# Rotating a matrix by 90 degrees: a new order of the output buffers, and a wait moved from TensorE to ScalarE

## The chip, the cores and the metric

The kernel runs on one core of one Trainium2 chip. The metric is the time of one execution on the device in microseconds (us), as the median of several runs. The engines that matter are TensorE (PE in the profile, with its weight loads as PEld), VectorE (DVE), ScalarE (ACT), GpSimd (POOL) and SyncE (SP). Transfers between the chip's main memory and the on-chip memory run on 16 DMA engines, which two queues share here: q1 holds what SyncE issues, q10 what ScalarE issues.

## The reference

The input `x` is a matrix of 8192 x 8192 float32 values, 268 MB, and `k` is 1. The result is the matrix turned by 90 degrees against the clock:

```
def reference(x, k):
    return np.rot90(x, k)
```

Element (r, c) of the input becomes element (8191 - c, r) of the output. There is no arithmetic: every value is read once and written once, but rows become columns.

## The kernel before, in words

**Tiling.** The input is cut into 16 macro tiles of 1024 rows by 4096 columns (`R`, `W`), counted by `kk`. A macro tile is loaded by 8 transfers of 128 full rows, 2 MB each (`m` counts loads over the whole run, 128 in all). It is written by 8 outputs (`n`, 128 in all), each 512 output rows by 1024 output columns, 2 MB each. `n % 8` is called the position of an output in its macro tile below.

**Path of the data.** A load lands in one of the buffers; VectorE copies it, reversed, into the `ring`, which holds one macro tile (63 slots of 128 x 512; a 64th piece, the corner, stays in its landing buffer). The copy of load t of the next macro tile overwrites the slots that output t of the present one has left. So VectorE, before it copies load m, waits until output m - 8 has been read out of the ring: `s_half` counts finished transposes on TensorE, `s_pool` finished outputs on GpSimd.

Outputs come by two ways. At positions 0, 2, 4 and 6 (`BY_PE`) TensorE transposes the 32 blocks of 128 x 128 into its accumulation memory `ps`, which has two halves of 128 x 2048, and ScalarE evicts them in three copies to an output buffer. At positions 1, 3, 5 and 7 (`moved`) VectorE transposes 32 x 32 blocks while it fills the ring, and the quarters of the blocks are moved to the output buffer by 16 copies: 2 by VectorE, 12 by GpSimd, 2 by ScalarE. The last of GpSimd's 12 waits for the other two engines' shares (`s_act`, `s_dve`). In the first and the last macro tile all outputs go by TensorE, and in the last but one position 7 does too.

**Buffers.** There are five buffers of 128 x 4096. After the start, numbers 0 and 1 (`LAND`) take loads in turn, and numbers 2, 3 and 4 (`OUTS`) take outputs. Which output takes which is said by `TURN`, one list for even macro tiles and one for odd ones. Eight outputs don't divide by three buffers, and the loops of VectorE, TensorE and GpSimd repeat every two macro tiles, so the order must repeat with 16 outputs. Read through, the lists before give a reuse distance (how many outputs back the same buffer was used) of 2 at position 0, 4 at position 1 and 3 elsewhere.

**Order of the work.** All orders and waits are written out by hand. SyncE issues the loads, each when the load two before has been taken out of its landing buffer (`taken`; for the last load of a macro tile this includes the corner, which TensorE transposes in the output at position 0). ScalarE issues every store right after the output's last eviction or move, and each store counts up `s_store` of its buffer. `room_for(wait, n)` waits until the last store from output n's buffer has landed. It is called by GpSimd, VectorE and ScalarE for outputs that are moved. For outputs of TensorE it is called by TensorE, ahead of the last transpose of the output's first part (`by_tensor`); ScalarE, which writes the buffer, is ordered behind it by `s_half`. ScalarE calls it itself only at position 7 (the corner) and for one output of the last macro tile.

Of the kernel before, what the change touches and what calls it, by code (L numbers as in the profile page):

```python
# [13 lines left out]
J = W // (G * P)  # L14
# [17 lines left out]
LAND = 2  # L32
OUTS = 3

LINE = 1024

TURN = [[1, 2, 0, 1, 2, 0, 1, 2], [1, 0, 2, 1, 0, 2, 1, 0]]
HEAD = 224


# [131 lines left out]
def kernel(tc: tile.TileContext, x: bass.AP, k: bass.AP, out: bass.AP):  # L172
# [7 lines left out]
    KK = len(macros)  # L180
    n_out = KK * J
# [17 lines left out]
    def in_quadrants(kk, j):  # L199
        return j not in by_pe(kk)  # L200

    moved = [in_quadrants(kk, js[0]) for kk, _, js, _ in outs]


    FIRST = [n_out - J, n_out - J + 1]
    parts, evicted, seen = {}, {}, 0
    for n, (kk, ts, js, blocks) in enumerate(outs):
# [4 lines left out]
        ends = [F // H, F - CH, F] if kk < KK - 1 else [F // H, end]  # L212
        if kk < KK - 1 and js[0] == J - 1:
            ends = [F // H, F // H + rows, F]
# [51 lines left out]
    def load_buf(m):  # L266
        if m < T:
            return m % (LAND + OUTS)
        return LAND + 2 if m == T else (m - T - 1) % LAND

    def out_buf(n):
        e = n - (KK * J - J)
        if e < 0:
            return LAND + TURN[n // J % 2][n % J]
        ends = [load_buf(n_load - 2)]
        ends += [LAND + i for i in range(OUTS)]
        ends += [load_buf(n_load - 1)]
        return ends[e % len(ends)]

    def once(e):  # L280
        seen = {}

        def wait(sem, n):
            if seen.get(sem, 0) < n:
                seen[sem] = n
                e.wait_ge(sem, n)

        return wait

    def room_for(wait, n):  # L290
        b = out_buf(n)
        stores = [i for i in range(n) if out_buf(i) == b]
        loads = [i for i in range(n_load) if load_buf(i) == b]
        if stores:
            wait(s_store[b], 16 * len(stores))
        elif loads:
            taken(wait, loads[-1])

    def taken(wait, m):
        kk, t = divmod(m, T)  # L300
        wait(s_rev, max(rev[m, j] for j in range(J)))
        if t == T - 1 and kk < KK - 1:
            wait(s_corner, kk + 1)  # L303
# [18 lines left out]
    for m in range(n_load):  # L322
        kk, t = divmod(m, T)
# [24 lines left out]
    def chunk(kk, t, js):  # L348
        if (kk, t, js[0]) == (KK - 1, T - 1, J - 1):
            return at(ring[:], 0, [[CH, 1], [1, CH]])  # L350
        places = [slot(kk, t, j) for j in js]
        assert max(places) < SLOTS
        return at(ring[:], places[0] * CH, [*strides(places, CH), [1, CH]])

    def moves(n, share):
        kk, ts, (j,), _ = outs[n]
        rows = len(ts) * P
        places = [slot(kk, t, j) for t in ts if (t, j) != (T - 1, J - 1)]
        ((step, tiles),) = strides(places, CH)
        for a, q in share:  # L360
            yield (
                at(
                    bufs[out_buf(n)][q * Q : q * Q + Q, :],
                    a * Q,
                    [[rows, G], [P, tiles], [1, Q]],
                ),
                at(
                    ring[a * Q : a * Q + Q, :],
                    places[0] * CH + q * Q,
                    [[P, G], [step, tiles], [1, Q]],  # L370
                ),
            )
# [19 lines left out]
    def load_in_turn(e, m, queue):  # L392
        if queue not in queues(m):
            return
        last = [i for i in range(m) if load_buf(i) == load_buf(m)]
        taken(e.wait_ge, last[-1])
        load(e, m, queue)
# [76 lines left out]
    def in_turn():  # L474
        for n in parts:
            if n == FIRST[0]:
                early, late = parts[n], parts[FIRST[1]]
                yield n, early[:2]
                yield FIRST[1], late[:1]
                yield n, early[2:]  # L480
                yield FIRST[1], late[1:]
            elif n != FIRST[1]:
                yield n, parts[n]

    def by_tensor(e):
        e.part(-1)
        wait = once(e)
        e.wait_ge(s_id, 2)
        used = {}
        for n, some in in_turn():  # L490
            kk, ts, js, blocks = outs[n]
            e.part(kk)
            rows = len(ts) * P
            order = [(part, f) for part in some for f in part[2]]
            if js[0] == 0 and kk < KK - 1:
                late = parts[n][-1]
                order.sort(key=lambda o: (o[0] == late, o[1] % rows, o[1]))
            last = dict(order)
            for part, f in order:
                _, h, cols = part  # L500
                j, off = blocks[f // rows]
                t = ts[f % rows // P]
                if kk < KK - 1 and js[0] == 0 and f == parts[n][-1][2][0]:
                    m = kk * T + T - 1
                    wait(s_rev, rev[m, J - 1])
                    wait(s_freed, kk)
                    for g in range(G):
                        i = e.transpose(
                            corner[:, g * P : g * P + P],
                            bufs[load_buf(m)][:, g * P : g * P + P],  # L510
                            ident,
                        )
                    i.then_inc(s_corner, 1)
                if n == KK * J - J and h:
                    wait(s_freed, KK - 1)
                if used.get(h, part) != part:
                    wait(s_ev, evicted[used[h][0]] + 1)
                wait(s_rev, rev[kk * T + t, j])
                if part == parts[n][0] and f == last[part] and n != FIRST[1]:
                    room_for(wait, n)  # L520
                to = cols.index(f) * P
                i = e.transpose(
                    ps[h][:, to : to + P],
                    chunk(kk, t, [j])[:, 0, off : off + P],
                    ident,
                )
                if f == last[part]:
                    i.then_inc(s_half, 1)
                    used[h] = part

    def by_scalar(e):
        e.part(-1)
        wait = once(e)
        e.wait_ge(s_id, 2)
        e.copy(scratch, ident[:, :1])
        for m in EARLY[LAND + OUTS :]:
            load_in_turn(e, m, nc.scalar)
        for n, (kk, ts, js, blocks) in enumerate(outs):
            e.part(kk)
            r0, c0 = macros[kk]  # L540
            rows = len(ts) * P
            b = out_buf(n)
            if moved[n] or n == FIRST[1] or (kk < KK - 1 and js[0] == J - 1):
                room_for(wait, n)
            todo = list(moves(n, pairs[BY_DVE + BY_POOL :])) if moved[n] else []
            for to, of in todo[:1]:
                e.copy(to, of)
            if kk < KK - 1 and js[0] == J - 1:
                e.wait_ge(s_corner, kk + 1)
                e.copy(  # L550
                    at(bufs[b][:], rows - P, [[rows, G], [1, P]]),
                    at(corner, 0, [[P, G], [1, P]]),
                ).then_inc(s_freed, 1)
            if moved[n]:
                for to, of in todo[1:]:
                    i = e.copy(to, of)
                i.then_inc(s_act, 1)
                e.wait_ge(s_pool, moved_until(n))
            else:
                for k, h, cols in parts[n]:  # L560
                    e.wait_ge(s_half, k + 1)
                    run, deep = len(cols) * P, 1
                    if cols[-1] - cols[0] >= run:
                        run = P * sum(f // rows == cols[0] // rows for f in cols)
                        deep = len(cols) * P // run
                    e.copy(
                        at(bufs[b][:], cols[0], [[rows, deep], [1, run]]),
                        at(ps[h][:], 0, [[run, deep], [1, run]]),
                    ).then_inc(s_ev, 1)
                e.wait_ge(s_ev, turned_until(n))  # L570
            groups = len(blocks)
            top = M - c0 - js[0] * CH - groups * P
            left = r0 + ts[0] * P
            e.dma_start(
                out=Place(out, top, groups * P, left, rows),
                in_=bufs[b][:, : groups * rows].rearrange("m (g f) -> m g f", f=rows),
            ).then_inc(s_store[b], 16)
# [12 lines left out]
    last = {out_buf(n): n for n in range(n_out)}  # L590
# [37 lines left out]
```

## Time and profile before

| | |
|---|---|
| median of 3 runs | 1261.35 us (1260.8 to 1262.37) |
| profiled execution | 1263.2 us, of which the profile's span is 1261.9 us |
| moved | 537.09 MB, mean 426 GB/s |
| queue q10 (stores and the first loads), share of 16 engines | 52.0% |
| queue q1 (loads) | 48.1% |
| GpSimd busy | 754.2 us (60%) |
| VectorE busy | 596.8 us (47%) |
| TensorE busy | 520.6 us (41%) |
| ScalarE busy | 391.0 us (31%) |
| TensorE waiting for a store | 297.8 us in 57 waits |
| GpSimd waiting for a store | 228.3 us in 41 waits |
| ScalarE waiting for a store | 52.5 us in 41 waits |
| a store of 2 MB, issue to landing (median) | 15.7 us |
| a load of 2 MB, issue to landing (median) | 15.8 us |

The profile shows one execution. Its slices cut the span in 40 equal parts; a window gives busy times of each engine in a stretch, with the number of instructions in brackets, then the clock granted to TensorE, the busy share of the 16 DMA engines and what they moved. A wait in brackets in the timeline is the idle time of an engine before an instruction, and behind the arrow stands what ended it. An instruction of the loops is put down to line 102 of the kernel, where a helper records all of them, so the groups are told apart by engine and tile name. The shares of the two queues add up to the whole span: an engine that is idle costs nothing unless it makes a queue run dry.

### The profile page before, as it was taken

What the parts mean: (1) busy time and instruction counts of PE and PEld (TensorE: products, weight loads), DVE (VectorE), ACT (ScalarE), POOL (GpSimd) and SP (SyncE); (2) the same over time, 40 slices, a digit from 0 to 9 for tenths busy, and PEclk for the clock granted to TensorE, in tenths of its full rate; (3) what the DMA queues carried; (4) which work ended last, traced back from release to release, by engine and by line L of the source; (5) the groups of instructions that cost most, each with busy time, mean ns of one, the idle gap of its engine ahead of it and who ended that gap; (6) DMA issues with size and microseconds to landing.
All of it is one profiled execution on the core that took longest, in us unless ns stands there. A gap on an engine that the chain in (4) does not pass through costs nothing.

```text
span 1261.9 us, 7238 instructions
## 1 busy us (share of the span) xinstructions
PE 520.6 (41%) x2388; PEld 436.2 (35%) x2388; DVE 596.8 (47%) x389; ACT 391.0 (31%) x339; POOL 754.2 (60%) x666
## 2 busy tenths in 40 slices
PE   1555444234433344433344344343443434434374
PEld 0444333233333233323233233332332333323364
DVE  2533555545455454554544555545555455454410
ACT  0333233222332333313323233232332322313254
POOL 0003566776668667686676766767767677677700
PEclk9975555656655556565666655555555555555577
DMA  9999999999999999999999999999999999999999
GB/s 398 420 428 423 410 430 412 430 429 413 431 427 428 431 430 428 431 431 428 430 431 430 428 430 431 430 428 431 430 428 430 431 430 428 431 430 428 429 421 385
DMA packets 36945, 537.09 MB, mean 426 GB/s; under 512 B 4160, under 2 KB 4160, under 8 KB 4160
## 3 DMA queue, kind: packets, MB, share of 16 engines
q10 hardware_dynamic: 19184, 278.93, 52.0%
q1 hardware_dynamic: 17744, 257.96, 48.1%
q8 instruction: 8, 0.13, 0.0%
q14 instruction: 9, 0.07, 0.0%
HBM read 268.44 MB, written 268.44 MB: 425 GB/s over the span
## 4 chain that ended last, share of the span: by engine, by line
DMA 75%; DVE 10%; issue 6%; ACT 4%; POOL 2%; PE 1%; ACTq 0%; DVEq 0%; SPq 0%; POOLq 0%
DMA buf<-in_x_dram 63%; DMA out_dram<-buf 12%; DVE ring L102 10%; ACT buf L102 4%; POOL buf L102 2%; PE ps L102 1%; DVE buf L102 1%; ACTq L102 0%; DVEq L99 0%; SPq L383 0%; SPq L411 0%; POOLq L149 0%; SPq L303 0%; POOLq L99 0%; SPq L406 0%
## 5 line engine op out<-in xcount | busy, mean ns | idle before, releaser
L102 POOL COPY buf<-ring 32x1024 f32<-32x1024 f32 (+1 forms) x660 | 753.5, 1142 | 437.6 <-DMA out_dram<-buf 228.3
L102 PE MATMUL ps<-head,ring 128*128 128x128 f32 x2328 | 507.8, 397 | 725.7 <-DMA out_dram<-buf 297.8
L102 PEld LDWEIGHTS ps<-head,ring 128*128 128x128 f32 x2328 | 423.4, 208 | 809.9 <-DMA out_dram<-buf 319.0
L102 ACT COPY buf<-ps 128x512 f32<-128x512 f32 (+3 forms) x227 | 277.8, 1288 | 796.3 <-POOL buf L102 459.9
L102 DVE COPY ring<-buf 128x2048 f32<-128x2048 f32 (+4 forms) x152 | 212.7, 1406 | 620.0 <-DMA buf<-in_x_dram 565.5
L102 DVE STREAM_TRANSPOSE ring<-buf 128x2048 f32<-128x2048 f32 (+1 forms) x112 | 246.3, 2199 | 0.0
L102 DVE COPY buf<-ring 32x1024 f32<-32x1024 f32 (+1 forms) x110 | 147.2, 1338 | 0.7
L102 ACT COPY buf<-ring 32x1024 f32<-32x1024 f32 (+1 forms) x110 | 111.7, 1016 | 57.8 <-DMA out_dram<-buf 47.7
L102 PE MATMUL ps<-head,buf 128*128 128x128 f32 x60 | 15.9, 420 | 0.0
L102 PEld LDWEIGHTS ps<-head,buf 128*128 128x128 f32 x60 | 13.0, 229 | 0.0
L102 DVE COPY buf<-buf 128x512 f32<-128x512 f32 x15 | 5.8, 386 | 0.0
L102 ACT ACT_TABLE_LOAD x1 | 1.3, 1283 | 3.4 <-PEq L411 3.4
L102 POOL MEMSET head<- 128x128 f32 x1 | 0.2, 204 | 2.9 <-POOLq L411 2.9
L102 POOL TENSOR_SCALAR_AFFINE_SELECT head<-head 128x128 f32<-128x128 f32 x1 | 0.3, 292 | 0.2 <-POOL head L102 0.2
L609 POOL MEMSET const-float32-0.0<- 128x1 f32 x1 | 0.1, 98 | 0.2 <-issue 0.2
L102 ACT COPY head<-head 128x1 f32<-128x1 f32 x1 | 0.2, 191 | 0.0
L609 POOL MEMSET const-bfloat16-1.0<- 128x1 bf16 x1 | 0.1, 101 | 0.0
L609 POOL MEMSET const-uint8-127<- 128x1 uint8 x1 | 0.1, 101 | 0.0
L609 POOL MEMSET const-float32-1.0<- 128x1 f32 x1 | 0.1, 98 | 0.0
## 6 DMA issues: line engine op xcount, KB each, us to landing
out_dram<-buf ACTq DMA_DIRECT2D x128, 2048.0 KB, 15.7
buf<-in_x_dram SPq DMA_DIRECT2D x121, 2048.0 KB, 15.8
buf<-in_x_dram ACTq DMA_DIRECT2D x3, 2048.0 KB, 16.9
buf<-in_x_dram SPq DMA_DIRECT2D x4, 1024.0 KB, 16.0
buf<-in_x_dram ACTq DMA_DIRECT2D x4, 1024.0 KB, 16.3
```

The lines of the kernel that those rows point to most:

```text
L102: i = getattr(e, self.name)(*self.args, **kwargs)
L609: nc = _bacc.Bacc("TRN2", target_bir_lowering=False, num_devices=1)
```

## The change

The lists in `TURN` are replaced. Read through, the new ones give distance 3 at positions 0 and 1, distance 2 at position 4, distance 4 at position 5 and 3 elsewhere. For outputs at position 4, in all macro tiles but the last (`tight`), `room_for` is no longer called by TensorE but by ScalarE, ahead of its first eviction of that output. In the last macro tile the three output buffers are taken in reverse order.

```
-TURN = [[1, 2, 0, 1, 2, 0, 1, 2], [1, 0, 2, 1, 0, 2, 1, 0]]
+TURN = [[1, 2, 0, 1, 0, 2, 1, 0], [2, 1, 0, 2, 0, 1, 2, 0]]
+TIGHT = 4
...
-        ends += [LAND + i for i in range(OUTS)]
+        ends += [LAND + i for i in reversed(range(OUTS))]
...
+    def tight(n):
+        return n < n_out - J and n % J == TIGHT
...
-                if part == parts[n][0] and f == last[part] and n != FIRST[1]:
+                if part == parts[n][0] and f == last[part] and n != FIRST[1] and not tight(n):
                     room_for(wait, n)
...
-            if moved[n] or n == FIRST[1] or (kk < KK - 1 and js[0] == J - 1):
+            if moved[n] or tight(n) or n == FIRST[1] or (kk < KK - 1 and js[0] == J - 1):
                 room_for(wait, n)
```

## The prediction

> **What bounds the kernel now.** I read the page's slices first, then busy time by windows, then the DMA queues in two short windows, then the timeline around them.
>
> Page, part 2 (40 slices of 31.5 us; DMA busy share, GB/s moved):
>
> ```profile
> DMA  9999999999999999999999999999999999999999
> GB/s 398 420 428 423 410 430 412 430 429 413 431 427 428 431 430 428 431 431 428 430 431 430 428 430 431 430 428 431 430 428 430 431 430 428 431 430 428 429 421 385
> ```
>
> DMA is busy throughout and moves about 430 GB/s wherever nothing disturbs it; 537.09 MB at 430 GB/s is 1249.0 us of the 1261.9 us span. So only the dips can be won: 12.9 us in all, start and end included. The windows place them (start:end, length, busy of PE, PEld, DVE, ACT, POOL, clock, DMA share, GB/s):
>
> ```profile
> 120.00:140.00 20.00, 12.35 (x55) 10.93 (x56) 8.87 (x6) 9.47 (x8) 7.84 (x8) 0.59 0.99 386
> 200.00:220.00 20.00, 12.07 (x54) 10.63 (x55) 9.49 (x7) 9.48 (x8) 12.05 (x11) 0.59 0.99 398
> 220.00:280.00 60.00, 18.48 (x80) 15.49 (x78) 30.90 (x21) 14.01 (x13) 43.35 (x39) 0.59 1.01 430
> 280.00:300.00 20.00, 12.39 (x57) 10.84 (x57) 9.90 (x6) 9.48 (x8) 11.42 (x10) 0.59 1.00 405
> 360.00:380.00 20.00, 12.47 (x57) 10.24 (x55) 9.76 (x6) 11.04 (x10) 11.99 (x12) 0.59 1.01 427
> 380.00:660.00 280.00, 108.10 (x470) 90.08 (x470) 143.65 (x92) 82.90 (x75) 198.36 (x176) 0.59 1.01 430
> ```
>
> Four dips, 78 to 80 us apart: the first outputs of macro tiles 1 to 4. Lost against 430 GB/s: 20 x (1 - 386/430) = 2.05 us, then 1.49, 1.16 and 0.14: 4.84 us. After 380 us there is none. The DMA share stands at 0.99 to 1.01 in a dip as outside it, so the share hides the loss and the GB/s shows it. Who stopped, by the queues (q10 carries the stores, q1 the loads), at 121.9 to 125.1 us and then at 127 to 131.4 us:
>
> ```profile
> q10 hardware_dynamic: 82, 1.33, 97.5%
> q1 hardware_dynamic: 1, 0.00, 0.0%
> ```
>
> ```profile
> q1 hardware_dynamic: 87, 1.43, 100.2%
> ```
>
> First the loads are dry and the stores alone run at 415 GB/s: almost nothing lost. Then the stores are dry, one load alone is in flight, and 324 GB/s flow: here the loss is made. The timeline names the cause (start, length, engine, operation, and in brackets the wait before):
>
> ```profile
> 122.60 0.69 PE L102 MATMUL ps<-head,ring 128*128 128x128 f32 x2 [9.17 <-DMA out_dram<-buf]
> 126.19 1.96 DVE L102 COPY ring<-buf 128x2048 f32<-128x2048 f32 x1 [9.16 <-PE ps L102]
> 126.84 0.55 ACTq L102 DMA_DIRECT2D out_dram<-buf  x1
> ```
>
> TensorE sits 9.17 us at the last transpose of output 8's first part until the store of output 6 lands (same buffer, two back). VectorE waits for TensorE (9.16 us) before it may write the next macro tile's load over the ring; the corner transposed behind the wait also holds a landing buffer, so SyncE issues its next load only at 124.23. Output 8's store goes out at 126.84.
>
> In the settled part nothing is lost. Four lines from there:
>
> ```profile
> 612.21 14.49 POOL L102 COPY buf<-ring 32x1024 f32<-32x1024 f32 x12 [5.80 <-DMA out_dram<-buf]
> 626.73 0.55 ACTq L102 DMA_DIRECT2D out_dram<-buf  x1
> 627.32 3.70 ACT L102 COPY buf<-ps 128x2048 f32<-128x2048 f32 x3 [13.15 <-POOL buf L102]
> 641.37 3.04 PE L102 MATMUL ps<-head,ring 128*128 128x128 f32 x13 [6.85 <-DMA out_dram<-buf]
> ```
>
> Output 0's store frees POOL for output 3 at 612.21; that store is issued at 626.73, and its landing frees TensorE for output 6 at 641.37. Stores land every 9.76 us (POOL's next room comes at 631.72, two stores after 612.21). So a store issued 14.6 us before its turn to land is in time.
>
> **The change, part by part.** Call the landing of a tile's output p L(p), 9.76 us apart.
>
> *Position 0 gets distance 3 (removes).* Output 8 then waits for output 5's store, which lands one turn before output 6's, near 112.8 us; the data for that transpose are in the ring only at about 113.1 (VectorE's copy of 112.62). The wait is covered by the load. The four dips go: -4.84 us at most. What is late next is position 1.
>
> *Position 1 falls from distance 4 to 3.* POOL starts at L(-2), as positions 3 and 7 do today: 14.5 us of copies, 14.6 us before its turn. No margin, but the same row at positions 3 and 5 runs at 430 GB/s. Position 5 takes over distance 4. Cost 0 in the settled part.
>
> *Position 4 waits at distance 2 on ScalarE (adds).* ScalarE issues store 3, then sits until L(2). From L(2): 0.4 us to start (the landing that frees POOL at 612.21 lets ScalarE start at 612.07; the last packet record of that store is at 611.7), 3.70 us for three evictions, 0.03 to the issue: L(2) + 4.1, that is 19.52 - 4.1 = 15.4 us before its turn, 0.8 us of margin against 14.6. Queued behind the wait on ScalarE: its two copies for position 5 (2.1 us, done by L(2) + 6.8), which POOL's last copy of position 5 needs. POOL starts that output as soon as position 3 is finished, L(0) + 15.1, and reaches the last copy 13.4 us later, at L(0) + 28.5; ScalarE is done at L(0) + 26.3. Store 5 has its turn to be issued at L(5) - 14.6 = L(0) + 34.2. Covered. TensorE no longer stops here; only its last four transposes wait for the first eviction, so VectorE's release for the load behind position 4 moves to L(2) + 0.4 + 1.9 + 1.1 = L(0) + 22.9. In the settled part load 8+p lands 13.3 us before store p (its ring copy starts at 628.09, store 59 frees TensorE at 641.37), so this load lands at 39.0 - 13.3 = 25.7: covered by 2.8 us. If that cover goes, loads are delayed by what is missing.
>
> *Tile 0 has the wait too.* The store of output 2 lands by 83.55 (TensorE's release there), so output 4 is issued at about 87.4 instead of 77.89; its landing frees the buffer of output 7 at 103.07 today: 15.7 us ahead, in time. VectorE's load write waits until about 86.0 instead of 83.35, and the load behind it goes out some 2.6 us late: about 1 us of dry loads, while the stores have three outputs queued. 0 by the 415 GB/s row, 0.5 if half the traffic is lost; I take 0.
>
> *The loads' head start (what is late next).* In tile 0 load 8+p lands 19.5 us before store p (load 12's copy starts at 83.35, beside the room that output 2 frees at 83.55). POOL's release at L(p-3) + 15.05 is 14.2 us before L(p), so at 19.5 VectorE is held 5 us; the head start must shrink. In tile 2 it is 15.5 us (236.47 against 251.93) and 220:280 runs at 430 GB/s: that is enough. Shrinking by 4.0 us costs 0 if the stores use all the bandwidth that the loads leave (the 97.5% row) and half of 4.0, 2.0 us, if they can't; down to 13.3, as before, up to 3.1 us. The stores of positions 1 and 3 have no margin to run ahead, which is nearer to the second: I take 1.5 us.
>
> *The last tile's buffers* come in reverse order; tile 14 ends on 2, 1, 0 instead of 2, 0, 1 at positions 5 to 7 (buffer numbers), so the distances stay 4. Cost 0. The added waits are one semaphore wait per tile on ScalarE; one on TensorE goes.
>
> Sum: -4.84 + 1.5 = -3.3 us. The profiled execution took 1263.2 us (span 1261.9), so it would take 1259.9; it stands 1.85 us above the median of 1261.35, which would become 1258.0, 0.27% less.
>
> **One rule against the row.** Between store issue at 126.84 and the first time q10 moves lie at least 4.6 us, since q10 is still silent in 127 to 131.4. The Trainium skill, "DMA: Bandwidth & Descriptors", section "Latency and other measured facts", gives about 0.6 us for the first byte on this path; no run here shows so short a time on the loaded store queue. By 0.6 us the new wait at position 4 would have some 4 us more margin and the sum stays -3.3 us, so only the first rival would fall.
>
> **The rivals.**
> Slower: ScalarE's wait at position 4 leaves the store queue dry in every tile. For it: 0.8 us of margin, and 4.6 us of silence once the queue is dry. Against: positions 3 and 5 live without loss on 14.6 us. It decides once the evictions start over 0.8 us after L(2) and the loads have no second transfer queued. Price: the dip of a later boundary, 1.16 us, in 15 tiles, 17.4, less 4.84: +12.6, 1274; with a third of the dip 1262.3.
> No difference that shows: the head start is lost in dips of the same size elsewhere (positions 1 and 3 of tiles 1 to 4), between 3.1 us and the whole 4.84 us given back: 1259.6 to 1261.4. For it: POOL has no margin there. Against: 140 to 200 us, where VectorE already waits on POOL at 156.91, ran at 430 GB/s.
> Full gain: the stores take all that the loads leave: 1256.5.
>
> **How the numbers follow.** About 0.2% (2.5 us) is what a measurement of this kernel tells from no change. Forecast 0.47 (1257 to 1258.8), full gain 0.13, no difference 0.27, the slower rival 0.13 (over 1263.9 in most of it). Hence faster 0.60, same 0.27, slower 0.13. Range 1255.8 to 1262.8: from a little beyond the full gain over all of the no-difference case to a mild form of the slower one.
>
> **What would show it.** 120:140, 200:220 and 280:300 at 425 GB/s or more; TensorE's 9.17 us wait near 122.6 gone and SyncE's issue of 124.23 near 117; ScalarE waiting some 4.3 us on a store before position 4 in each tile (about 60 us in all, against 52.5 us on stores now). Wrong would be: a window after 140 us below 425 GB/s, or dips at position 1 or 4 with q10 silent.

## The result, and the profile after

The changed kernel takes 1260.22 us (median of 20 runs, 1259.53 to 1261.38), the kernel before, run beside it, 1262.28 us (1260.55 to 1269.13). The ratio is 0.9982, 95% interval 0.9973 to 0.9990: 0.18% faster, 2.3 us, with 1.3 to 3.4 us in the interval. The kernel before has a long tail of slower executions, up to 1269.13 us; the two medians alone give 0.9984, 2.1 us. The forecast was 1258.0 us with a range of 1255.8 to 1262.8, 0.27% faster. So the sign was right, the time lies in the range, and the gain is two thirds of the forecast; it is beyond the interval of this measurement, but just inside the 0.2% that the prediction drew as its bound of "no difference".

The profiled execution has a span of 1259.3 us against 1261.9. Part 2 of its page (40 slices, DMA busy share and GB/s):

```profile
DMA  9999999999999999999999999999999999999998
GB/s 399 414 429 430 429 428 430 428 430 430 428 430 429 429 431 428 431 429 429 431 428 431 429 429 430 429 429 431 428 431 424 430 430 429 429 423 426 427 427 375
```

The dips of the first third (423, 410, 412, 413 before) are gone: from the third slice to the thirtieth the row stands at 428 to 431. New are 424, 423 and 426 in the last quarter, while the last slice but one rose from 421 to 427 and the last one fell from 385 to 375. The same windows as in the prediction, with the last ones added:

```profile
55.00:120.00 65.00, 33.06 (x224) 28.37 (x224) 23.10 (x16) 25.92 (x22) 0.00 (x0) 0.78 1.00 429
120.00:140.00 20.00, 7.09 (x31) 6.29 (x32) 9.72 (x6) 4.82 (x5) 14.03 (x12) 0.50 1.01 431
140.00:200.00 60.00, 24.56 (x111) 21.00 (x110) 29.70 (x21) 19.97 (x19) 42.66 (x37) 0.59 1.01 429
200.00:220.00 20.00, 7.50 (x34) 6.46 (x34) 10.21 (x6) 6.12 (x7) 14.55 (x14) 0.59 1.00 428
280.00:300.00 20.00, 7.70 (x34) 6.99 (x35) 10.20 (x6) 5.78 (x5) 14.61 (x13) 0.66 1.00 427
380.00:660.00 280.00, 103.52 (x457) 87.72 (x457) 142.65 (x94) 82.69 (x74) 198.99 (x174) 0.56 1.01 430
940.00:1200.00 260.00, 102.53 (x452) 87.90 (x453) 125.62 (x86) 81.75 (x73) 182.71 (x156) 0.56 1.01 427
```

The boundary windows read 431, 428 and 427 GB/s where they read 386, 398 and 405. The window 940 to 1200 us reads 427 where the kernel before reads 429; over 260 us that is 1.2 us lost again. The line of the kernel before:

```profile
940.00:1200.00 260.00, 103.98 (x434) 86.22 (x435) 126.84 (x87) 79.93 (x71) 181.37 (x156) 0.54 1.01 429
```

The first boundary in the timeline of the changed kernel (its loops are put down to line 103):

```profile
115.63 0.90 PE L103 MATMUL ps<-head,ring 128*128 128x128 f32 x3 [5.89 <-DVE ring L103]
118.83 0.33 SPq L387 DMA_DIRECT2D buf<-in_x_dram  x1
120.25 0.55 ACTq L103 DMA_DIRECT2D out_dram<-buf  x1
125.02 1.61 DVE L103 COPY ring<-buf 128x2048 f32<-128x2048 f32 x1 [6.32 <-DMA buf<-in_x_dram]
```

TensorE now waits for the data that VectorE brings, not for a store; SyncE's load goes out at 118.83 instead of 124.23, output 8's store at 120.25 instead of 126.84, and VectorE waits for a load's landing, not for TensorE.

Position 4 in the settled part:

```profile
624.76 0.55 ACTq L103 DMA_DIRECT2D out_dram<-buf  x1
629.64 3.70 ACT L103 COPY buf<-ps 128x2048 f32<-128x2048 f32 x3 [17.37 <-DMA out_dram<-buf]
633.37 0.55 ACTq L103 DMA_DIRECT2D out_dram<-buf  x1
```

ScalarE issues store 3 at 624.76, is through with that at 625.3 and starts output 4 at 629.64: 4.3 us of waiting, the size that was forecast. (The 17.37 us in brackets count from ScalarE's last copy, so they hold the wait for GpSimd as well.) The packet records put the landing of output 2's store at 629.62 us and that of output 4's at 649.24, 15.9 us behind its issue. The forecast had 15.4, as it gave the start 0.4 us, where 0.02 us were needed.

### The profile page after: what moved, and what is told of

Same layout as the page of the kernel before. It is cut to its first block, busy times and chain, and to the rows that moved or that the text cites. A ratio compares the mean times of both kernels' runs of the same rounds, so it can differ in the third digit from the quotient of the medians.

```text
span 1259.3 us, 7229 instructions
## 1 busy us (share of the span) xinstructions
PE 495.7 (39%) x2388; PEld 422.8 (34%) x2388; DVE 589.3 (47%) x389; ACT 392.2 (31%) x339; POOL 765.0 (61%) x666
## 4 chain that ended last, share of the span: by engine, by line
DMA 73%; DVE 12%; issue 6%; ACT 3%; POOL 2%; PE 1%; DVEq 0%; ACTq 0%; SPq 0%
DMA buf<-in_x_dram 68%; DVE ring L103 11%; DMA out_dram<-buf 5%; ACT buf L103 3%; POOL buf L103 2%; PE ps L103 1%; DVEq L100 0%; ACTq L103 0%; DVE buf L103 0%; SPq L387 0%; DVEq L144 0%; SPq L415 0%; SPq L410 0%
## 5 line engine op out<-in xcount | busy, mean ns | idle before, releaser
L103 POOL COPY buf<-ring 32x1024 f32<-32x1024 f32 (+1 forms) x660 | 764.3, 1158 | 423.0 <-DMA out_dram<-buf 380.7
L103 PE MATMUL ps<-head,ring 128*128 128x128 f32 x2328 | 482.2, 385 | 730.6 <-ACT buf L103 381.5
L103 PEld LDWEIGHTS ps<-head,ring 128*128 128x128 f32 x2328 | 412.2, 203 | 797.7 <-ACT buf L103 410.6
L103 DVE COPY buf<-ring 32x1024 f32<-32x1024 f32 (+1 forms) x110 | 139.8, 1271 | 0.7
## 6 DMA issues: line engine op xcount, KB each, us to landing
buf<-in_x_dram SPq DMA_DIRECT2D x121, 2048.0 KB, 15.5
```

Source lines behind the costliest of these rows:

```text
L103: i = getattr(e, self.name)(*self.args, **kwargs)
```

## The experiments

Some numbers come from no view but from the packet records of the trace: when a queue is dry, when a packet of the instruction queue moves, and landings. Each transfer of 2 MB ends there in 16 semaphore writes, taken here as one for each of the 16 DMA engines, and it has landed with the last of them. "Spread" below is the time from the first to the last of the 16 for one store.

**The changed kernel again**

> The changed kernel once more, for a second profile. In the first one the windows up to 380 us gained some 4.2 us on the kernel before, as the theory of the prediction has it (the dips at the macro tile boundaries go), but only 2.6 us were left at the end: stores landed every 9.76 us up to about 470 us and every 9.78 to 9.84 us, with one step of 10.4, behind that. Theory A (chance of one execution: the place where the even pace ends moves about, since the kernel before has the same slow-down from about 730 us on): the second profile has the end of the even pace elsewhere, and the gain at the end lies anywhere between 2 and 4 us. Theory B (the change itself brings it, by the stores of positions 1 and 3 that have no margin): the even pace ends near 470 us again, and the gain at the end is again 2.3 to 2.8 us.

Measured: 1260.00 us, ratio 0.9985 (0.9976 to 0.9994), span 1258.6 us. From 120 us on its windows are 428 to 430 GB/s up to 940 us and 428 from 940 to 1200. The even pace of 9.76 us ends at the same place as in the first profile: the last landing of the stores falls behind the other 15 from about 530 us on, with a spread of 2.0 us at 530, 3.4 at 609, and 5.5 us at 922. Theory B as to the place. Its gain at the end, 2.3 to 2.8 us, was missed: the span is 3.3 us under that of the kernel before, inside theory A's 2 to 4. Nor is the cause what theory B says: two runs below with the old order, where position 1 has distance 4, read 427 and 428 GB/s from 940 to 1200 us as well.

**The new order, TensorE waits at position 4**

```
     def tight(n):
-        return n < n_out - J and n % J == TIGHT
+        return False
```

> The new order of buffers, but TensorE waits for the room at position 4, as at 0, 2 and 6. Theory A (what cost time was that the wait stood at the boundary, where TensorE held back the corner and with it the next load): at position 4 no corner is behind TensorE's wait, store 4 goes out about 0.7 us later than in the changed kernel and VectorE is released about 0.7 us later, so the gain stays nearly whole: 1.5 to 2.5 us faster than before, no window after 140 us below 425 GB/s. Theory B (a wait of TensorE at distance 2 stops VectorE's ring write wherever it stands): the dips come back near position 4 of macro tiles 0 to 3, 386 to 405 GB/s in a window of 20 us, and the time is that of before within 0.5 us.

Measured: 1260.42 us, ratio 0.9988 (0.9979 to 0.9997), against 0.9985 for the changed kernel on the same chip. 140 to 200 us run at 429, 200 to 220 at 431, 280 to 300 at 428 GB/s. Theory A: a wait of TensorE at distance 2 costs nothing where no corner stands behind it. Who waits at position 4 makes no difference that the time shows.

**The old order, ScalarE waits at position 0**

```
+TURN = [[1, 2, 0, 1, 2, 0, 1, 2], [1, 0, 2, 1, 0, 2, 1, 0]]
+TIGHT = 0
...
+        return J <= n < n_out - J and n % J == TIGHT
```

> The old order of buffers, so distance 2 stays at position 0, but there ScalarE waits for the room (from macro tile 1 on) and TensorE doesn't. Theory A (TensorE's stop was the cause): ring and corner are free as soon as the data are there, SyncE's load goes out near 117 us, and the dips of 120 to 140 and 200 to 220 us go: 1.5 to 3.5 us faster than before. Theory B (the late store itself was the cause, as output 8 can't leave before output 6's store has landed, whoever waits): output 8's store goes out at 126 us as before, 5 us after the queue would want it, and at least half of the dips stays: 0 to 1 us faster.

Measured: 1260.13 us, ratio 0.9984 (0.9975 to 0.9993): the whole gain without the rotation. Its first boundary (timeline):

```profile
116.92 0.33 SPq L387 DMA_DIRECT2D buf<-in_x_dram  x1
122.41 3.70 ACT L103 COPY buf<-ps 128x2048 f32<-128x2048 f32 x3 [14.53 <-DMA out_dram<-buf]
125.48 1.48 DVE L103 COPY ring<-buf 128x2048 f32<-128x2048 f32 x1 [8.58 <-PE ps L103]
126.14 0.55 ACTq L103 DMA_DIRECT2D out_dram<-buf  x1
```

Its windows, with the columns of those above:

```profile
120.00:140.00 20.00, 9.96 (x51) 8.68 (x51) 8.39 (x6) 9.57 (x8) 8.64 (x8) 0.62 1.01 429
200.00:220.00 20.00, 12.19 (x51) 10.19 (x51) 9.95 (x6) 9.95 (x10) 10.88 (x10) 0.50 1.01 430
```

This is the run that tells most. VectorE still waits 8.58 us for TensorE and writes the ring at 125.48 (126.19 before), and store 8 still leaves at 126.14 (126.84 before). Nearly everything that was late is late still, and the dip is gone: 429 where it was 386. One thing is early: SyncE's load, at 116.92 instead of 124.23, since the corner is no longer behind TensorE's wait. So theory A is right in the time and the load, but not in that the ring would be free early; and theory B's late store is there and costs nothing. The two queues from 127 to 131.4 us tell why. The prediction shows this stretch for the kernel before, with q1 alone:

```profile
q10 hardware_dynamic: 89, 1.23, 65.8%
q1 hardware_dynamic: 56, 0.69, 36.6%
```

With the load in the queue, output 7's store shares the bandwidth with it and lands at 132.14 us. In the kernel before it had the bandwidth to itself while the loads were dry, and landed at 127.27, 4.35 us before output 8's store moved its first data (131.62, packet records). Store 8 is as late in both, but only there did it find an empty queue.

**The corner first**

The kernel before, with one line changed:

```
-                if kk < KK - 1 and js[0] == 0 and f == parts[n][-1][2][0]:
+                if kk < KK - 1 and js[0] == 0 and f == parts[n][0][2][-1]:
```

> The kernel before, but at position 0 TensorE transposes the corner ahead of the transposes that wait for the room. So SyncE's load goes out as soon as the landing buffer is read (near 117 instead of 124 us), while VectorE's write over the ring still waits for TensorE until about 126 us. Theory A (the load held back by the corner is what makes the loads dry): the dips of the first boundaries go by half or more, 1 to 2 us faster than before. Theory B (the ring write alone holds the next load but one just as long, so that the loads go dry one transfer later): 120 to 140 us stays below 415 GB/s and the time is that of before within 0.7 us.

Measured: 1260.41 us beside 1262.71 us, ratio 0.9977 (0.9965 to 0.9990). The gain is 2.3 us by the medians and 2.9 by the ratio, a little over theory A's 1 to 2. Its windows:

```profile
120.00:140.00 20.00, 10.79 (x53) 8.74 (x53) 8.49 (x6) 9.52 (x8) 8.74 (x9) 0.60 1.00 408
200.00:220.00 20.00, 10.86 (x50) 8.93 (x51) 9.99 (x7) 9.55 (x9) 12.04 (x11) 0.59 1.00 428
280.00:300.00 20.00, 10.79 (x51) 8.96 (x51) 9.84 (x6) 10.44 (x10) 11.89 (x11) 0.67 1.01 428
```

The second and third dip are gone, the first is halved (1.0 us lost instead of 2.05): theory A. What is left of the first, 408 GB/s, is theory B's: the ring write still waits until 127.51 us, and in the packet records the loads run dry one transfer later, for 3.1 us from 132.0 on. With the buffers, the waits and the late store as before, moving four small transposes ahead of the wait brings as much as the whole change, within the intervals. So most of the dips was made by the load that the corner withheld, at a moment when the store was late too.

**Macro tile 0 without distance 2**

```
-            return LAND + TURN[n // J % 2][n % J]
+            return LAND + (TURN[n // J % 2] if n >= J else [1, 0, 2, 1, 0, 2, 1, 0])[n % J]
...
-        return n < n_out - J and n % J == TIGHT
+        return J <= n < n_out - J and n % J == TIGHT
```

> The changed kernel, but macro tile 0 takes its buffers in the order 1, 0, 2, 1, 0, 2, 1, 0, so that no output of it has distance 2 and ScalarE does not wait there; from macro tile 1 on all is as in the changed kernel. In the changed kernel load 14 of macro tile 1 went out 3.5 us later than before, and the load queue was dry for 2.15 us near 81 us in the packet records. Theory A (that cost some 0.7 us and did nothing else): 0.4 to 0.9 us faster than the changed kernel. Theory B (the loads have to give up their head start anyway, and here they do it at the least price): the dry load comes in macro tile 1 instead, at positions 1 and 3, where POOL's release is late, and the time is that of the changed kernel within 0.3 us or up to 1.5 us longer.

Measured: 1260.19 us, ratio 0.9984 (0.9975 to 0.9993), that of the changed kernel. The stretch of tile 0 (55 to 120 us) rose from 429 to 431 GB/s and the next (120 to 140) fell from 431 to 426. Theory B: the price of the head start moves, and does not go. In the packet records the loads are now dry for 2.9 us from 141.5 us and 2.1 us from 161.7. (The dry stretch of the changed kernel that the expectation puts near 81 us lies near 92 us.)

**Evictions at position 4 made longer**

```
+                    for _ in range(1 if tight(n) and k == parts[n][0][0] else 0):
+                        e.copy(
+                            at(bufs[b][:], cols[0], [[rows, deep], [1, run]]),
+                            at(ps[h][:], 0, [[run, deep], [1, run]]),
+                        ).then_inc(s_pad, 1)
+                        padded += 1
+                        e.wait_ge(s_pad, padded)
```

once, and twice in the second run.

> The changed kernel with one eviction of 128 x 2048 done twice at each position 4 (1.87 us more on ScalarE after the room is there). Store 4 then leaves 13.5 us ahead of its turn to land instead of 15.4. Theory A (the prediction's margin of 0.8 us against 14.6 is real): the store queue runs dry by about 1.1 us in each of 15 macro tiles, the loads take up part of it, 1 to 6 us slower than the changed kernel. Theory B (loads and stores cover each other, and the slowest DMA engine sets the pace anyway): the time of the changed kernel within 0.5 us.

> As before, with that eviction done three times (3.74 us more). Store 4 leaves 11.7 us ahead of its turn, and VectorE's release for the load behind it comes 3.7 us later, 3 us after that load has landed. Theory A: both queues run dry at position 4 of every macro tile, 0.7 us or more lost each, at least 10 us slower than the changed kernel. Theory B: within 2 us of the changed kernel, as the loads' head start settles at another value and the traffic stays near 430 GB/s.

Measured: once more, 1261.62 us, ratio 0.9986 (0.9975 to 0.9998), against 0.9985 for the changed kernel on another chip; the median is 1.4 to 1.6 us and the span 1.5 to 2.2 us longer than the changed kernel's. Twice more, 1267.84 us, ratio 1.0029 (1.0011 to 1.0047), span 1266.0 us. The windows of the first:

```profile
55.00:120.00 65.00, 32.46 (x219) 28.81 (x220) 22.68 (x16) 26.30 (x22) 0.00 (x0) 0.78 1.00 421
380.00:660.00 280.00, 101.03 (x469) 85.74 (x467) 140.12 (x94) 90.15 (x78) 199.75 (x175) 0.59 1.01 430
```

and of the second:

```profile
55.00:120.00 65.00, 31.91 (x222) 28.11 (x223) 23.35 (x16) 29.45 (x25) 0.00 (x0) 0.80 0.99 412
380.00:660.00 280.00, 98.26 (x475) 85.05 (x473) 140.55 (x92) 97.83 (x83) 195.90 (x175) 0.61 1.01 429
940.00:1200.00 260.00, 92.27 (x428) 79.94 (x428) 126.74 (x87) 93.02 (x77) 184.29 (x158) 0.59 1.01 425
```

1.87 us more at position 4 cost nothing in the settled part (430 GB/s) and about 1.2 us once, in tile 0 (65 x 8/430). By the median that is inside theory A's 1 to 6 us, by the ratio it is theory B's; theory A's loss in each of 15 macro tiles isn't there. 3.74 us cost 5.6 us by the ratios (0.9985 to 1.0029) and 7.6 by the medians, between the two theories: 2.6 us of it in tile 0 (65 x 17/430, against the changed kernel), the rest in later windows.

The margin of 0.8 us was not the point from which it costs. In the packet records of the second run the store queue falls silent for 1.5 to 1.7 us in each macro tile from 400 to 650 us, and the loads then for 2.3 to 3.0 us, yet 380 to 660 us stands at 429 GB/s: each queue fills the other's short silence. A silence of 4.8 us, in the kernel before at 126.85, or of 5.1 us, in this run at 97.8, is not filled (324 and 318 GB/s). What makes the rest of this run's cost, behind 660 us above all, is not shown.

**The transfers alone**

All work of TensorE, VectorE and GpSimd and the evictions are left out; loads wait only for the landing two back, stores for the landing three back.

> Leaves out all that turns the data: no work on TensorE, VectorE and GpSimd, and the output is not the reference's. The same 128 loads and 128 stores of 2 MB from the same queues and buffers; each load waits only for the landing two loads back in its buffer, each store only for the landing three stores back. The changed kernel and three variants of it all came out at 1260.0 to 1260.4 us, whatever was done to their waits, and in all of them one of the 16 semaphore writes of each transfer falls behind the other 15 from about 550 us on (2.7 us behind near 1080 us; in the kernel before from 730 us on, 1.1 us behind near 1080 us). Theory A (the slowest of the 16 DMA engines is the floor, and the changed kernel stands on it): 1258.5 to 1260.5 us, and the same engine falls behind by 2 us or more. Theory B (the changed kernel still loses time to its waits, 1.5 us for the loads' head start and the rest at the end): 1254 to 1257 us.

Measured: 1255.26 us (1255.12 to 1255.35), ratio 0.9932 (0.9914 to 0.9950). Theory B by the time: the changed kernel stands 4.9 us above what the transfers need with these waits. But the slow DMA engine of theory A is missing here: the spread stays at 0.5 to 0.8 us through the run. So what makes one engine late comes with the work beside the transfers. Three runs add that work back, engine by engine.

**GpSimd, VectorE, TensorE with ScalarE beside the transfers**

> The transfers alone (1255.3 us), and beside them GpSimd copies 32 x 1024 blocks inside the ring without pause, 960 of them, bound to no transfer; the output is not the reference's. In the transfers alone the last of the 16 landings of a store comes 0.5 to 0.8 us after the first, all the way; in the changed kernel this spread grows from 2 us at 530 us to 5.5 us at 1080 us. Theory A (GpSimd's traffic in the on-chip memory slows one DMA engine): the spread grows to 3 us or more while GpSimd works, 1258 us or longer. Theory B (not GpSimd; another engine, or the waits themselves): spread under 1 us, 1255 to 1256 us.

> The transfers alone, and beside them VectorE without pause: 230 times a reversed copy and a block transpose of 128 x 2048 and a copy of 32 x 1024 inside the ring, about 1.15 ms of work, twice the kernel's share; the output is not the reference's. Theory A (VectorE's traffic slows one DMA engine): spread of the landings 3 us or more, 1258 us or longer. Theory B (not VectorE): spread under 1 us, 1255 to 1256 us.

> The transfers alone, and beside them 2400 transposes on TensorE from the ring and, before each store, two evictions of 128 x 2048 on ScalarE into the ring, as many as in the kernel; the output is not the reference's. Theory A (these engines' traffic or power slows a DMA engine): spread 3 us or more, 1258 us or longer. Theory B (not these): spread under 1 us, 1255 to 1256 us. If all three variants follow theory B, the slow DMA engine comes from the waits, that is from a transfer queue that is not filled early enough, and not from the other engines' memory traffic.

Measured: 1259.23, 1258.98 and 1259.79 us; ratios 0.9976, 0.9974 and 0.9980. All three by theory A, by nearly the same amount (3.7 to 4.5 us over the transfers alone), whatever the work. Their spreads reach 4.7, 4.5 and 5.7 us. With GpSimd they grow in steps of 0.5 to 0.6 us that follow the packets of the instruction queue q14 (75 to 1053 us), with VectorE in steps of 0.6 to 0.9 us that follow theirs (95, 267, 444, 622 and 795 us). With TensorE, whose 2400 transposes are a loop, the spread grows evenly from 1.0 us at 92 us to 5.0 us at 301, where TensorE works, with no step at the one packet there (139.7 us). One step of 0.7 us stands beside the packet at 618.6; those at 455.6, 768.5 and 1080.2 left the spread as it was. So code may explain the first two runs, and not most of the third. The last run keeps GpSimd's code and takes the data traffic away:

**The code without its work**

```
-                out=at(ring[q * Q : q * Q + Q, :], 54 * CH + a * Q, [[R, G], [P, T], [1, Q]]),
-                in_=at(ring[a * Q : a * Q + Q, :], (n % 8) * CH + q * Q, [[P, G], [J * CH * 3 // 4, T], [1, Q]]),
+                out=at(ring[q * Q : q * Q + Q, :], 54 * CH + a * Q, [[1, 1]]),
+                in_=at(ring[a * Q : a * Q + Q, :], (n % 8) * CH + q * Q, [[1, 1]]),
```

> The variant with GpSimd's 960 copies, but each copies one element per partition, so that next to no data is moved on the chip and the program is as long; the output is not the reference's. In that variant the last landing of a store fell behind the others in some eight steps, 0.6 us at a time, in step with the packets of the instruction queue q14 (75, 215, 355, 494, 634, 775, 913 and 1053 us in the packet records). Theory A (the loading of program code on one DMA engine sets it back): all steps come within the first 150 to 200 us, as the instructions run through at once, the spread is 4 us or more from there on, and the time is 1258.5 to 1259.5 us, as with full copies. Theory B (the traffic of the copies in the on-chip memory does it): spread under 1 us, 1255 to 1256 us.

Measured: 1259.01 us, ratio 0.9975 (0.9966 to 0.9985). Theory A: with GpSimd copying one element per partition the time is that of the full copies. (The transfers alone ran on another chip; the profiled spans, 1257.6 and 1254.0 us, and the spreads within each run say the same as the medians.) The instruction queue of its page, beside that of the transfers alone (first line here, second there):

```profile
q14 instruction: 10, 0.08, 0.0%
```

```profile
q14 instruction: 2, 0.02, 0.0%
```

Eight packets of 8 KB more, now at 49 to 259 us (one each 30 us, where theory A had the last at 200 at most). The spread takes a step of about 0.6 us beside each of them, from 0.4 us to 4.6 us at 262 us, and has no step of size after. The packets came earlier than with the full copies, and the steps with them. What the spread does to the end is seen in windows of 2 us at the end (start:end, length, busy of DVE and POOL, clock, DMA share, GB/s):

```profile
1251.00:1253.00 2.00, 0.00 (x0) 0.00 (x0) 1.00 0.77 328
1253.00:1255.00 2.00, 0.00 (x0) 0.00 (x0) 1.00 0.08 33
1255.00:1257.00 2.00, 0.00 (x0) 0.00 (x0) 1.00 0.06 25
```

A share of 0.06 is one of 16 engines: by the landings of the last store fourteen are done by 1253.6 us, the next at 1254.5, and the kernel waits until 1257.5 for the last. In the transfers alone the share is 0.89 in 1251:1253 and 0.00 after. The changed kernel ends in a like way, less sharply (the five engines' busy time, then clock, share and GB/s):

```profile
1253.00:1255.00 2.00, 0.00 (x0) 0.00 (x0) 0.00 (x0) 0.00 (x0) 0.00 (x0) 0.50 0.94 401
1255.00:1257.00 2.00, 0.00 (x0) 0.00 (x0) 0.00 (x0) 0.00 (x0) 0.00 (x0) 0.50 0.29 123
1257.00:1259.00 2.00, 0.00 (x0) 0.00 (x0) 0.00 (x0) 0.00 (x0) 0.00 (x0) 0.50 0.04 16
```

Its last store has fifteen of its landings between 1255.2 and 1257.15 us and the last at 1259.23. In the kernel before the fifteenth comes at 1260.97 and the last at 1261.84. So fifteen landings came 3.8 us earlier than before, and the kernel's end 2.6 us.

## Why the prediction was right or wrong

**The dips go, -4.84 us.** Right. Against 430 GB/s the four windows lost 4.84 us before and lose 0.3 us now: 4.5 us won.

**Their cause.** Half right. The prediction named two chains behind TensorE's wait, the ring write and the corner, and put the ring first. With the ring write as late as before and only the corner freed, the old order loses 1.0 us in one dip instead of 4.84 in four (the run with the corner first), or none (ScalarE waiting at position 0). It was mostly the withheld load that made the late store costly: while the loads were dry, the store before it landed early, and the late one found the queue empty: 4.8 us passed from its issue to its first data. So the rotation was not needed for the gain, and neither was ScalarE at position 4. The changed kernel and the two edits of the old order that free the corner gain 1.9 to 2.9 us by the ratios; their intervals overlap, so they can't be ranked.

**Position 4 on ScalarE, 0 us.** Right, with the right wait (4.3 us) and nearly the right distance from issue to landing (15.9 us against 15.4). The price at which it would turn was wrong: 1.9 us of delay cost nothing in the settled part, and 3.7 us cost 5.6 to 7.6 us over the whole run. The row of 14.6 us tells about when the store queue falls silent, and not what that costs, since the loads fill a short silence. On that the slower rival rested.

The Trainium skill, "DMA: Bandwidth & Descriptors", section "Latency and other measured facts", gives about 0.6 us for the first byte. By that figure, an estimate, the margin would have been some 4 us more, 4.8 us in all. The runs are on the row's side: in the kernel before the store queue's silences end 3.9 to 4.8 us after the store's issue, and in the run with 3.74 us more those of 1.5 us or more end 2.7 to 4.9 us after it.

**Tile 0, 0 us.** Nearly right. SyncE's load there left at 90.56 instead of 86.83 and the load queue was dry for 2.2 us in the packet records (from the start of its last packet to that of the next), twice what was thought; the stretch of 55 to 120 us lost 0.15 us (429 for 430).

**The loads' head start, +1.5 us.** Mis-sized. Loads land 15.9 us ahead of the stores in the settled part, against 15.5 in the forecast, so the new balance was right (landings in the packet records). Its price was not: 55 to 380 us lose 0.15 to 0.3 us more than the 430 of before outside the dips. Most of the shift, from 19.7 to 16.7 us, happened in tile 0, while stores were queued to use the bandwidth; that is the lower bound (0) of that term, and the row that showed it (97.5% on q10) had been at hand.

**The missing term, +1.5 us.** The prediction held the stretch behind 380 us to be the same in both kernels. It isn't. From the windows, against 430 GB/s: 940 to 1200 us lose 1.8 us now and 0.6 before, and from 1200 us to the end 4.2 and 3.9 us. The start of this execution was 0.2 us slower as well. The sum is -4.5 + 0.15 + 1.2 + 0.3 + 0.2 = -2.65, against 2.6 us between the spans. The first term was a little too good, the second 1.35 us too dear, the missing one 1.5 us: that the last two nearly cancel is luck. The sum holds for this pair of executions alone; the second profile of the changed kernel has a span 0.7 us shorter, with 428 GB/s from 940 to 1200 us.

**What the missing term is.** The last of a store's 16 landings falls behind the other 15 and the kernel ends with it: at the end by 2.1 us, against 0.9 before. In the stripped kernel it is shown that loading GpSimd's code does this, and what it costs: eight packets of 8 KB, 3.75 us. That is not shown for the changed kernel: both kernels have the same number of such packets (nine on q14, and eight of 16 KB on q8), and one step of the spread there lies beside a packet of q14 at 563 us. The slow growth behind that (some 0.03 us per output, with no packet near) is not explained and stays open, as does the even growth in the stripped run with TensorE at work. So does why the kernel before has less of it (spread 4.2 us at 1080 us, against 5.5). That the stalls at its boundaries gave the late engine time to catch up is not enough: its spread does fall there, from 5.0 to 2.6 us at the third, but at 530 us, 150 us after its last stall, both kernels stand at 1.9 to 2.0 us, and they part only behind that.

**The rivals.** Full gain: not reached; the transfers alone need 1255.3 us, and with one or two engines' code and work beside them they end at 1259 to 1260. No difference: wrong in its mechanism (no dips elsewhere), though its range of times holds the result, which the forecast's own, 1257 to 1258.8, does not. Slower: didn't happen, and would have needed between 1.9 and 3.7 us more on ScalarE.

## What to carry to other kernels

When two queues share one resource, a short silence of one can be filled by the other (1.5 us here). Look for the long ones, here a dry load queue that emptied the store queue next, and then for the one instruction that withholds the next transfer: four transposes that stood behind a wait that was not theirs, worth as much in one moved line, within the noise, as the whole new order of buffers. A stall that is removed is worth only what the end of the run keeps of it: check whether the slowest of the parallel DMA engines, not their mean, sets the end, by the DMA share in the last microseconds. And measure the transfers alone early, since that tells how much is left to win at all.

## What the runs showed of the hardware

Loading code can cost DMA time on one engine: 960 one-element copies on GpSimd, with eight packets of 8 KB in the instruction queue, made 256 transfers of 2 MB take 1259.0 us instead of 1255.3, though the packets carry 0.01% of the bytes. The work of GpSimd or VectorE, 0.96 to 0.99 ms of it, beside the transfers cost no more than that code (1259.2 and 1259.0 us). Not every such packet costs: with TensorE and ScalarE at work, four of five left the spread as it was.

A transfer counts as landed when the last of its 16 writes is there: ScalarE went on at 629.64 us, with the fifteenth landing at 628.62 and the last at 629.62. In the stripped kernels such a delay stayed to the end (spread 4.6 us from 262 us on). In the real ones it can shrink, as in the changed kernel from 4.2 us at 103 us to 2.3 at 179.

Loads and stores together move 430 GB/s, and stores alone for 3.2 us about as much (415), but one load alone for 4.4 us moved 324. A store issued into an empty store queue moved its first data 3.9 to 4.8 us later in the kernel before.
